# An encoder layer in split fp32: the mixer's weights split in the first input stage and kept in DRAM

## Chip, cores, metric

The kernel runs on one core of a Trainium2 chip. The metric is the device time of one execution in microseconds, the median of several.

## What is computed

One layer on x (1024 tokens, 1024 features, fp32) and a condition vector c. Three sub-layers follow each other, each

```
x <- LayerNorm(ALPHA * x + w * (1 + gate(c)) * f(x * (1 + scale(c)) + shift(c)))

1. f = SwiGLU FFN, w = 1/2:      (silu(h @ Wg) * (h @ Wu)) @ W_out,   2816 hidden columns
2. f = mixer, w = 1:             proj = h @ mix_w_in  (1024 x 2560: glu_a, glu_b, q, k, v)
       conv_out = silu(LN(depthwise_conv31(glu_a * sigmoid(glu_b))))        512 features
       attn_out = 4 heads of differential attention, partial rotary         512 features
       f = concat(conv_out, attn_out) @ mix_w_out                           1024 x 1024
3. f = SwiGLU FFN, w = 1/2
```

All shifts, scales and gates are one product of silu(c) with w_ada (1024 x 9216).

## The kernel before

Products run in a split form: each fp32 operand x is stored as `hi` (x rounded to fp32r, an ACT cast, L139) and `lo` (x minus hi, a subtract, L140), and a product is three matmuls, hi with hi, lo with hi, hi with lo. The helper `split` makes such a pair; its subtract is on DVE unless another engine is named.

The stages, in the order of time: (a) the first input stage (`in_phase`, profile lines L305 to L473): 22 steps j, each of which makes 128 hidden columns of gate and up. A step is a Strassen-Winograd product with seven products of half size (A11, A12, A22, S1 to S4 in the names). Its weights are loaded as tiles `ra` and `rb`, four sums of tiles are made (`sf`, L329 to L332), and both are split (`ah`/`al` and `sh`/`sl`). The sums of the activations (`r_0t` and so on, L264 to L272) are made on POOL, chunk by chunk (0 to 3), as the condition's columns for the chunk come in (`ada0a`, DVE, L708 and L710) and `A`, `B` (L724, L725) are made from them. (b) The first output stage (`out_phase`, L563). (c) The mixer's projections: glu (L891), then k, q, v (`proj_tok`), while DVE runs the convolution (L910). (d) Attention, 32 iterations, each of scores, softmax (maximum on DVE, L1036; exponential on ACT, L1038), `combine` (DVE makes `c`, POOL scales and adds the two maps, L1089 and L1090), transposes of p and the product with v. (e) The output projection (L1274). (f) The second FFN's two stages.

A list scheduler places the instructions of each engine in one order; each engine then executes its queue in order and waits at the head. A tile pool with `bufs` tiles of a tag hands a tile out again when its last readers are done.

What the change touches: in stage (b) a hook makes the second gate, `gate1` (`ada_gate`: eight accumulations on DVE, L151 and L153, for each of two halves). In (c) the weights of mix_w_in are loaded raw (`glur`, `kr`, `qr`, `vr`, 20 tiles of 128x1024) and split by ACT and DVE. In (d) and (e) `out_weights` loads the eight tiles of mix_w_out (`mor`), multiplies each by gate1 (L1060; tiles 0, 1, 6, 7 on POOL, 2 to 5 on DVE) and splits it (`moh`, `mol`). In (a) a hook after each step from j=2 on makes parts of the condition's columns and gates (`ada`, DVE).

Of the kernel before, what the change touches and what calls it, by code (L numbers as in the profile page):

```python
# [48 lines left out]
def layer_kernel(ctx, tc, a, out):  # L49
# [239 lines left out]
    def new_ops():  # L289
# [4 lines left out]
        "ra": ([P, 3, 4, P], 2), "rb": ([P, 4, P], 2), "ah": ([P, 3, 4, P], 2), "al": ([P, 3, 4, P], 2),  # L294
# [11 lines left out]
    def in_load(wp, s, w_in, j):  # L306
        rp = raw_pool.get(s, wp)
        ra = rp.tile([P, 3, 4, P], F32, tag="ra", bufs=2, name=f"ra{s}_{j}")
        rb = rp.tile([P, 4, P], F32, tag="rb", bufs=2, name=f"rb{s}_{j}")
# [5 lines left out]
        return ra, rb  # L315

    def in_gate(wp, s, j, raws):
        ra, rb = raws
        ah = wp.tile([P, 3, 4, P], F32R, tag="ah", bufs=2, name=f"ah{s}_{j}")
        al = wp.tile([P, 3, 4, P], F32R, tag="al", bufs=2, name=f"al{s}_{j}")  # L320
        split(ah, al, ra)
        return {n: (ah[:, i], al[:, i]) for i, n in enumerate(("A11", "A12", "A22"))}

    def in_sums(wp, s, j, raws, left, eng=V, order=(0, 1)):
        ra, rb = raws
        if s == 2 and order == (0, 1) and j in (1, 2):
            eng = G
        sf = [wp.tile([P, 2, 4, P], F32, tag="sf", bufs=2, name=f"sf{s}_{j}_{i}") for i in range(2)]
        eng.tensor_tensor(sf[0][:, 0], rb, ra[:, 2], ALU.add)  # L329
        eng.tensor_tensor(sf[0][:, 1], sf[0][:, 0], ra[:, 0], ALU.subtract)  # L330
        eng.tensor_tensor(sf[1][:, 0], ra[:, 0], rb, ALU.subtract)
        eng.tensor_tensor(sf[1][:, 1], ra[:, 1], sf[0][:, 1], ALU.subtract)  # L332
        for i in order:
            sh = wp.tile([P, 2, 4, P], F32R, tag="sh", bufs=3, name=f"sh{s}_{j}_{i}")
            sl = wp.tile([P, 2, 4, P], F32R, tag="sl", bufs=3, name=f"sl{s}_{j}_{i}")
            split(sh, sl, sf[i])
            for e in range(2):
                left[f"S{2 * i + e + 1}"] = (sh[:, e], sl[:, e])
# [172 lines left out]
    def out_phase(s, wp, w_out, gd, gate, xs, done, after, hook):  # L511
# [111 lines left out]
        for i, (n, k) in enumerate(steps):  # L623
# [15 lines left out]
            if k < cut:  # L639
# [9 lines left out]
                hook(n, k)  # L649
# [16 lines left out]

    x_in = a["x"][0]
    with pool("p1a") as wp:
        in_tags(wp, "ra rb ah al sf sh sl")
# [138 lines left out]
    rows = tc.alloc_tile_pool(name="rows", bufs=1, reuse_waits="tile", side="right")  # L808
    gate1 = rows.tile([P, D], F32, tag="gate1", name="gate1")
    mix_in = a["mix_w_in"][0]  # L810
    spill1 = [dram.tile([P, D], F32, name=f"spill1_{t}", tag="spill1", bufs=NT) for t in range(NT)]
    hm = [[None, None] for _ in range(KD)]
    with pool("p1b") as wp:
# [24 lines left out]

        def load_glu(wp, i, th, tl, nb, tr, nr):
            ws = []  # L840
            for kh in range(2):
                raw = wp.tile([P, 4, 2 * P], F32, tag=tr, bufs=nr, name=f"glur{i}{kh}")
                src = mix_in[kh * H : (kh + 1) * H, :].rearrange("(k p) n -> p k n", p=P)
                SY.dma_start(raw[:, :, 0:P], src[:, :, i * P : (i + 1) * P])
                SY.dma_start(raw[:, :, P : 2 * P], src[:, :, H + i * P : H + (i + 1) * P])
                if th:
                    hi = wp.tile([P, 4, 2 * P], F32R, tag=th, bufs=nb, name=f"gluh{i}{kh}")
                    lo = wp.tile([P, 4, 2 * P], F32R, tag=tl, bufs=nb, name=f"glul{i}{kh}")
                else:
                    hi, lo = slot(f"gluh{i}{kh}", (P, 4, 2 * P)), slot(f"glul{i}{kh}", (P, 4, 2 * P))  # L850
                split(hi, lo, raw)
# [615 lines left out]
```

## Time and profile before

| | us |
|---|---|
| median of 3 runs (lowest, highest) | 1918.4 (1914.31, 1918.53) |
| profiled execution, its time | 1915.77 |
| its span, first to last instruction | 1914.0 |
| TensorE busy in it | 1828.2 |
| VectorE busy | 1463.4 |
| ScalarE busy | 773.6 |
| GpSimd busy | 325.6 |

The span is that of the profiled execution. PE is TensorE's matmuls, DVE is VectorE, ACT is ScalarE, POOL is GpSimd, SP is the engine that issues most transfers. Busy time counts the work, not the issue of transfers by SP; time in which PE is not busy is where it waits. The mean granted clock of TensorE is 0.979.

### The profile page before, as it was taken

What the parts mean: (1) busy time and instruction counts of PE and PEld (TensorE: products, weight loads), DVE (VectorE), ACT (ScalarE), POOL (GpSimd) and SP (SyncE); (2) the same over time, 40 slices, a digit from 0 to 9 for tenths busy, and PEclk for the clock granted to TensorE, in tenths of its full rate; (3) what the DMA queues carried; (4) which work ended last, traced back from release to release, by engine and by line L of the source; (5) the groups of instructions that cost most, each with busy time, mean ns of one, the idle gap of its engine ahead of it and who ended that gap; (6) DMA issues with size and microseconds to landing.
All of it is one profiled execution on the core that took longest, in us unless ns stands there. A gap on an engine that the chain in (4) does not pass through costs nothing. (4 is left out here: it accounts for less than half of the span.)

```text
span 1914.0 us, 23141 instructions
## 1 busy us (share of the span) xinstructions
PE 1828.2 (96%) x8562; PEld 1513.0 (79%) x8562; DVE 1463.4 (76%) x1982; ACT 773.6 (40%) x1233; POOL 325.6 (17%) x259
## 2 busy tenths in 40 slices
PE   5899999999999999999999889979999999999997
PEld 5688888888888878878788677857888888888886
DVE  8867667766698878999888768688777565569888
ACT  3423333332445442133277664353333333354540
POOL 3200000000000020057667541260000000000001
PEclk7899999999999999999999999989999999999999
DMA  8536555442885324111000014125555333188432
GB/s 254 165 99 208 163 161 175 158 149 83 296 301 165 113 61 163 46 35 33 11 2 1 12 45 154 67 67 170 168 172 177 121 110 127 39 285 281 127 121 72
DMA packets 203696, 246.76 MB, mean 129 GB/s; under 512 B 14122, under 2 KB 124831, under 8 KB 203582
## 3 DMA queue, kind: packets, MB, share of 16 engines
q1 hardware_dynamic: 200234, 235.81, 38.6%
q0 software_dynamic: 2112, 7.34, 1.0%
q10 hardware_dynamic: 1236, 2.13, 0.3%
q8 instruction: 67, 1.10, 0.2%
q14 instruction: 47, 0.39, 0.1%
HBM read 188.08 MB, written 57.15 MB: 128 GB/s over the span
## 5 line engine op out<-in xcount | busy, mean ns | idle before, releaser
L563 PE MATMUL fo<-wr,gl 128*128 128x512 f32 x1848 | 422.5, 390 | 0.5 <-DVE pv L606 0.4
L563 PEld LDWEIGHTS fo<-wr,gl 128*128 128x128 f32 x1848 | 346.2, 188 | 74.8 <-DVE pv L606 0.8
L140 DVE TENSOR_TENSOR sl<-sf,sh 128x1024 fp32r<-128x1024 f32 x87 | 109.3, 1257 | 118.5 <-ACT sh L139 118.5
L139 ACT CAST sh<-sf 128x1024 fp32r<-128x1024 f32 x88 | 92.7, 1054 | 210.0 <-issue 35.8
L910 DVE SCALAR_TENSOR_TENSOR cacc<-u,convw,cacc 128x1009 f32<-128x1009 f32 (+14 forms) x120 | 151.5, 1324 | 0.2
L373 POOL DMA_DIRECT2D gd<-gf x8 | 4.6, 573 | 824.4 <-DVE gf L439 823.9
L140 DVE TENSOR_TENSOR gl<-gr,gl 128x512 fp32r<-128x512 f32 x148 | 102.3, 698 | 7.2 <-ACT gl L139 5.8
L139 ACT CAST gl<-gr 128x512 fp32r<-128x512 f32 x148 | 90.5, 618 | 23.2 <-DMA gr<-gd 16.5
L153 DVE SCALAR_TENSOR_TENSOR ada<-adaw,c_act,ada 128x512 f32<-128x512 f32 x98 | 73.3, 748 | 32.9 <-DMA adaw<-in_w_ada_dram 31.9
L215 POOL TENSOR_TENSOR rr<-rv,mhalf 128x1 f32<-128x1 f32 x24 | 21.8, 909 | 410.3 <-DVE rv L213 408.9
L1036 DVE TENSOR_REDUCE mx<-sc 128x1 f32<-128x1024 f32 x64 | 76.3, 1216 | 19.2 <-PE sc L1034 19.2
L1038 ACT ACTIVATE p<-sc,mx 128x1024 f32<-128x1024 f32 x64 | 71.6, 1122 | 45.1 <-DVE mx L1036 44.9
L139 ACT CAST ah<-ra 128x1536 fp32r<-128x1536 f32 x44 | 65.1, 1479 | 58.0 <-DMA ra<-in_ffn_w_in_dram 14.3
L140 DVE TENSOR_TENSOR al<-ra,ah 128x1536 fp32r<-128x1536 f32 x44 | 77.1, 1752 | 1.6 <-ACT ah L139 1.4
L401 ACT ACTIVATE gf<-gf 128x512 f32<-128x512 f32 x44 | 27.8, 632 | 120.8 <-DVE gf L400 114.9
L139 ACT CAST wr<-wa 128x512 fp32r<-128x512 f32 x66 | 41.2, 624 | 74.3 <-PE fo L563 73.7
L140 DVE TENSOR_TENSOR wr<-wa,wr 128x512 fp32r<-128x512 f32 x66 | 45.5, 690 | 26.6 <-ACT wr L139 26.3
L891 PE MATMUL glu<-hm,gluh 128*128 128x512 f32 x256 | 65.6, 391 | 0.0
L1090 POOL TENSOR_TENSOR p<-p,p 128x1024 f32<-128x1024 f32 x27 | 65.0, 2408 | 1.8
L139 ACT CAST wr<-wb 128x512 fp32r<-128x512 f32 x66 | 40.2, 620 | 60.4 <-PE fo L563 49.7
L1107 PE MATMUL av<-vf,aT 128*128 128x128 f32 x512 | 63.2, 277 | 1.0 <-ACT cacc L1172 1.0
L1107 PEld LDWEIGHTS av<-vf,aT 128*128 128x128 f32 x512 | 60.6, 194 | 1.5 <-ACT cacc L1172 1.3
(3490 smaller groups left out, 4735.9 us busy)
## 6 DMA issues: line engine op xcount, KB each, us to landing
gr<-gd SPq DMA_DIRECT2D x148, 256.0 KB, 3.4
ra<-in_ffn_w_in_dram SPq DMA_DIRECT2D x132, 256.0 KB, 3.7
adaw<-in_w_ada_dram SPq DMA_DIRECT2D x56, 512.0 KB, 3.9
gd<-gf SPq DMA_DIRECT2D x102, 256.0 KB, 2.1
rb<-in_ffn_w_in_dram SPq DMA_DIRECT2D x44, 256.0 KB, 3.7
wb<-in_ffn_w_out_dram SPq DMA_DIRECT2D x44, 256.0 KB, 5.0
wa<-in_ffn_w_out_dram SPq DMA_DIRECT2D x44, 256.0 KB, 5.1
gd<-s SPq DMA_DIRECT2D x40, 256.0 KB, 2.0
```

The source lines that it names most:

```text
L139: a = S.copy(hi, x)
L140: b = eng.tensor_tensor(lo, x, hi.bitcast(F32), ALU.subtract)
L153: V.scalar_tensor_tensor(acc, raw[:, jj], c_act[:, n : n + 1], acc, ALU.mult, ALU.add)
L215: G.tensor_tensor(r, v, mhalf[:, 0:1], ALU.pow)
L401: S.activation(c0, c0, AF.Silu)
L563: PE.matmul(ps, lhsT=g[:, x, ts_], rhs=w[:, y], start=n in (1, 2, 3) and k == i == 0, stop=k == NK - 1 and i == 2, skip_group_check=n not ...
L891: PE.matmul(q[2 * m + h], lhsT=w[:, m * P : (m + 1) * P], rhs=hm[k][h][:, x], start=k == 0 and n == 0, stop=k == KD - 1 and n == 2,)
L910: V.scalar_tensor_tensor(acc[:, lo_t:hi_t], u[:, lo_t + sh : hi_t + sh], convw[:, i, jj : jj + 1], acc[:, lo_t:hi_t], ALU.mult, ALU.add,)
L1036: V.tensor_reduce(mx_, ps, axis=AX.X, op=ALU.max, negate=True)
L1038: S.activation(pe, ps, AF.Exp, bias=mx_, accum_out=sm[:, e : e + 1])
L1090: last = G.tensor_tensor(p0, p0, p1, ALU.add)
L1107: PE.matmul(ps[:, 0:P], lhsT=aT[:, kt], rhs=vf[kt][:, h * P : (h + 1) * P], start=kt == 0, stop=kt == 7)
```

## The change

The split of the mixer's weights is taken out of stages (c) to (e) and made in stage (a), in 56 units of 128x512 (40 of mix_w_in, 16 of mix_w_out): POOL's queue loads the weights, for mix_w_out DVE multiplies them by gate1, ACT makes the rounded part, DVE subtracts in place, POOL's queue stores both parts to DRAM (`mwi`, `mwo`). Two tiles (`mw`) are in turn; a step makes two units where it also works on the condition's columns, and four otherwise. The mixer then loads hi and lo from DRAM with SP, two transfers for one. gate1 is made in stage (a) at j=3 and 5, and the late constants are loaded at j=7 in place of 3. The four tile sums of a step in stage (a) are made in place in one tile of four (`r4`), so that the separate `sf` tiles go, and they come after `al` has read the tile. The pools for hi and lo in (c) grow from 4 to 5 tiles.

```diff
     def in_load(wp, s, w_in, j):
         rp = raw_pool.get(s, wp)
-        ra = rp.tile([P, 3, 4, P], F32, tag="ra", bufs=2, name=f"ra{s}_{j}")
-        rb = rp.tile([P, 4, P], F32, tag="rb", bufs=2, name=f"rb{s}_{j}")
+        if s == 0:
+            r4 = rp.tile([P, 4, 4, P], F32, tag="r4", bufs=2, name=f"r4{s}_{j}")
+            ra, rb = r4[:, 0:3], r4[:, 3]
...
     def in_sums(wp, s, j, raws, left, eng=V, order=(0, 1)):
...
+        if s == 0:
+            for i in order:
+                if i == 0:
+                    eng.tensor_tensor(ra[:, 2], rb, ra[:, 2], ALU.add)
+                    eng.tensor_tensor(rb, ra[:, 0], rb, ALU.subtract)
+                    eng.tensor_tensor(ra[:, 0], ra[:, 2], ra[:, 0], ALU.subtract)
+                else:
+                    eng.tensor_tensor(ra[:, 1], ra[:, 1], ra[:, 0], ALU.subtract)
...
-            split(sh, sl, sf[i])
+            split(sh, sl, r4[:, i::2] if s == 0 else sf[i])
...
+        gate1_at = (3, 5)
...
+        def mix_part(src, dst, gate=None):
+            t = wp.tile([P, 2, H], F32, tag="mw", bufs=2, name="mw")
+            G.dma_start(t[:, 0], src)
+            if gate is not None:
+                V.tensor_tensor(t[:, 0], t[:, 0], gate, ALU.mult)
+            S.copy(t[:, 1].bitcast(F32R), t[:, 0])
+            V.tensor_tensor(t[:, 0].bitcast(F32R), t[:, 0], t[:, 1], ALU.subtract)
+            G.dma_start(dst, t)
...
         def hook(j):
-            if j == 3:
-                late_consts(wp, "ra", 2)
+            if j in gate1_at:
...
+                todo[j + 1] = ada_gate(wp, raw_slot, 1, 1.0, mods["gate1"], n)
+            if j == 7:
+                late_consts(wp, "r4", 2)
...
+            for _ in range(2 if j in cols_at + gate_at + gate1_at else 4):
+                if units:
+                    src, dst, *hs = units.pop(0)
+                    mix_part(src, dst, mods["gate1"][:, hs[0]] if hs else None)
...
-        def hook(gi, j):
-            if (gi, j) in ((5, 3), (7, 3)):
-                todo1[(7, 2) if gi == 5 else (4, 1)] = ada_gate(wp, raw_ar, 1, 1.0, gate1, int(gi == 7))
...
-                raw = wp.tile([P, 4, 2 * P], F32, tag=tr, bufs=nr, name=f"glur{i}{kh}")
...
-                split(hi, lo, raw)
+                for g in range(2):
+                    src = mwi[g][kh * H : (kh + 1) * H].rearrange("(k p) x n -> p k x n", p=P)
+                    for x, w in enumerate((lo, hi)):
+                        SY.dma_start(w[:, :, g * P : (g + 1) * P].bitcast(F32), src[:, :, x, i * P : (i + 1) * P])
...
-                SY.dma_start(raw, src)
...
-                split(hi, lo, raw)
...
+                src = mwi[col // H][q * 256 : (q + 1) * 256].rearrange("(k p) x n -> p k x n", p=P)
+                for x, w in enumerate((lo, hi)):
+                    SY.dma_start(w.bitcast(F32), src[:, :, x])
...
-    def out_weights(wp, j, eng=V, tag="raw", size=D):
-        raw = wp.tile([P, size], F32, tag=tag, bufs=2, name=f"mor{j}")[:, 0:D]
-        SY.dma_start(raw, a["mix_w_out"][0, j * P : (j + 1) * P, :])
-        eng.tensor_tensor(raw, raw, gate1, ALU.mult)
+    def out_weights(j):
         mo_w[j] = slot(f"moh{j}", (P, D)), slot(f"mol{j}", (P, D))
-        split(*mo_w[j], raw)
+        for w, x in zip(mo_w[j], (1, 0)):
+            SY.dma_start(w.bitcast(F32).rearrange("p (h n) -> p h n", h=2), mwo[j][:, :, x])
...
-            last = combine(i)
+            combine(i)
...
-                with tc.issue_after(last):
-                    out_weights(wp, (i - 22) // 4, G)
+                out_weights((i - 22) // 4)
```

The order of instructions, first on POOL at the start of the program. The names end in buffer numbers; `r0_0t12` and `r0_0t34` are the tile sums of the activations' chunk 0, which the profile shows as `r_0t`. Before:

```order
masks.py:197 MEMSET ident_73 128x128
L87 MEMSET mhalf_80 128x4
masks.py:199 ISA
masks.py:199 AFFINE_SELECT ident_73<-ident_73 128x128
L264 TENSOR_TENSOR r0_0t12_278<-h0_0_1_267,h0_0_0_255 128x512
L265 TENSOR_TENSOR r0_0t12_278<-h0_0_1_267,r0_0t12_278 128x512
L271 TENSOR_TENSOR r0_0t34_285<-h0_0_1_267 128x512
L272 TENSOR_TENSOR r0_0t34_285<-h0_0_0_255,r0_0t12_278 128x512
```

Of the change, from the same row:

```order
masks.py:197 MEMSET ident_73 128x128
L87 MEMSET mhalf_80 128x4
L814 DMA mw_965<-in_mix_w_in_dram 128x512
masks.py:199 ISA
masks.py:199 AFFINE_SELECT ident_73<-ident_73 128x128
L819 DMA mwi0_99<-mw_965 128x1024
L814 DMA mw_970<-in_mix_w_in_dram 128x512
L814 DMA mw_1129<-in_mix_w_in_dram 128x512
L819 DMA mwi0_99<-mw_970 128x1024
L819 DMA mwi0_99<-mw_1129 128x1024
L814 DMA mw_1134<-in_mix_w_in_dram 128x512
L264 TENSOR_TENSOR r0_0t12_292<-h0_0_1_281,h0_0_0_269 128x512
```

Three stores and four loads (`mw`) stand ahead of the first sum, and one more load ahead of the second; a load of a tile waits until the store of two units ago has landed, and a store waits for its subtract.

Then on DVE at the same place, from the making of `A` and `B` for chunk 0 on (`sf` and `r4` hold the sums of the first step's weights, `h` is the activation). Before:

```order
L724 TENSOR_TENSOR B0_107<-ada0p0_193,bada_84 128x2
L725 SCALAR_TENSOR_TENSOR A0_106<-ada0p0_193,bada_84 128x2
L329 TENSOR_TENSOR sf0_0_0_385<-rb0_0_225,ra0_0_224 128x512
L331 TENSOR_TENSOR sf0_0_1_386<-ra0_0_224,rb0_0_225 128x512
L330 TENSOR_TENSOR sf0_0_0_385<-sf0_0_0_385,ra0_0_224 128x512
L140 TENSOR_TENSOR al0_0_235<-ra0_0_224,ah0_0_234 128x1536
L740 TENSOR_SCALAR h0_0_0_255<-hT0_0_0_246,A0_106,B0_107 128x512
L332 TENSOR_TENSOR sf0_0_1_386<-ra0_0_224,sf0_0_0_385 128x512
L740 TENSOR_SCALAR h0_0_1_267<-hT0_0_1_258,A0_106,B0_107 128x512
```

Of the change:

```order
L743 TENSOR_TENSOR B0_122<-ada0p0_208,bada_84 128x2
L744 SCALAR_TENSOR_TENSOR A0_121<-ada0p0_208,bada_84 128x2
L140 TENSOR_TENSOR al0_0_249<-r40_0_239,ah0_0_248 128x1536
L818 TENSOR_TENSOR mw_970<-mw_970 128x512
L336 TENSOR_TENSOR r40_0_239<-r40_0_239 128x512
L759 TENSOR_SCALAR h0_0_0_269<-hT0_0_0_260,A0_121,B0_122 128x512
L759 TENSOR_SCALAR h0_0_1_281<-hT0_0_1_272,A0_121,B0_122 128x512
L337 TENSOR_TENSOR r40_0_239<-r40_0_239 128x512
L818 TENSOR_TENSOR mw_1129<-mw_1129 128x512
L338 TENSOR_TENSOR r40_0_239<-r40_0_239 128x512
L340 TENSOR_TENSOR r40_0_239<-r40_0_239 128x512
```

`al0_0` moved ahead of the sums, which now write into its operand, and two subtracts of units (L818) stand among them; one more stands before this piece and others follow.

Last on POOL in the attention, around the tile `mor0` (`p` are the attention maps, `c` their factors, `r44` the factor of an output tile). Before:

```order
L1090 TENSOR_TENSOR p220_8760<-p220_8760,p221_8769 128x1024
L1126 TENSOR_TENSOR r44_8803<-ss4_8568,mhalf_80 128x4
L1060 TENSOR_TENSOR mor0_8875<-mor0_8875,gate1_3723 128x1024
L1089 TENSOR_SCALAR p231_8837<-p231_8837,c123_8884 128x1024
L1090 TENSOR_TENSOR p230_8828<-p230_8828,p231_8837 128x1024
L1089 TENSOR_SCALAR p241_8905<-p241_8905,c124_8963 128x1024
```

Of the change:

```order
L1119 TENSOR_TENSOR p220_8969<-p220_8969,p221_8978 128x1024
L1155 TENSOR_TENSOR r44_9012<-ss4_8777,mhalf_80 128x4
L1118 TENSOR_SCALAR p231_9046<-p231_9046,c123_9090 128x1024
L1119 TENSOR_TENSOR p230_9037<-p230_9037,p231_9046 128x1024
L1118 TENSOR_SCALAR p241_9111<-p241_9111,c124_9169 128x1024
L1119 TENSOR_TENSOR p240_9102<-p240_9102,p241_9111 128x1024
```

The multiply of `mor0` is gone, and the rest stands as it did.

## Rows read from the trace of the kernel before

**Rows 1.** Page, busy us (share of the span) and instructions.

```profile
PE 1828.2 (96%) x8562; PEld 1513.0 (79%) x8562; DVE 1463.4 (76%) x1982; ACT 773.6 (40%) x1233; POOL 325.6 (17%) x259
```

**Rows 2.** Windows: length, busy of each engine (instructions), clock, DMA share, GB/s.

```profile
22.00:52.00 30.00, 19.90 (x71) 15.95 (x71) 29.64 (x45) 12.93 (x17) 11.32 (x8) 0.56 0.73 229
106.00:490.00 384.00, 383.39 (x1718) 316.48 (x1717) 261.54 (x370) 124.58 (x159) 0.00 (x0) 1.00 0.48 151
490.00:640.00 150.00, 150.00 (x663) 123.94 (x662) 124.53 (x198) 77.55 (x137) 4.72 (x7) 1.00 0.74 243
850.00:950.00 100.00, 94.32 (x431) 77.99 (x430) 95.03 (x79) 24.23 (x47) 75.29 (x55) 0.97 0.09 27
1050.00:1200.00 150.00, 129.47 (x769) 110.37 (x769) 112.38 (x146) 90.75 (x184) 57.84 (x33) 0.95 0.20 67
```

**Rows 3.** DVE timeline, 0 to 60 us: start, length, work [idle before].

```profile
15.62 1.75 DVE L140 TENSOR_TENSOR al<-ra,ah 128x1536 fp32r<-128x1536 f32 x1
...
20.82 0.95 DVE L708 TENSOR_SCALAR ada0a<-ada,c_act 128x256 f32<-128x256 f32 x1 [1.04 <-DMA ada<-in_w_ada_dram]
```

**Rows 4.** POOL timeline, 0 to 80 us.

```profile
19.00 1.28 POOL L264 TENSOR_TENSOR r_0t<-h,h 128x512 f32<-128x512 f32 x1 [17.70 <-ACT h L251]
```

**Rows 5.** DMA, 0 to 90 us: 40 slices; issues with KB, us to landing.

```profile
GB/s 18 278 360 350 294 316 349 349 346 348 348 349 349 348 277 11 0 250 354 95 0 256 305 293 351 312 259 146 0 0 0 0 39 226 209 134 292 116 44 23
...
ada<-in_w_ada_dram SPq DMA_DIRECT2D x16, 512.0 KB, 8.4
```

**Rows 6.** Page, costliest groups: busy, mean ns | idle before.

```profile
L373 POOL DMA_DIRECT2D gd<-gf x8 | 4.6, 573 | 824.4 <-DVE gf L439 823.9
L140 DVE TENSOR_TENSOR gl<-gr,gl 128x512 fp32r<-128x512 f32 x148 | 102.3, 698 | 7.2 <-ACT gl L139 5.8
```

**Rows 7.** DMA issues, the whole span: KB each, us to landing.

```profile
gd<-gf SPq DMA_DIRECT2D x102, 256.0 KB, 2.1
...
spill<-x POOLq DMA_DIRECT2D x8, 512.0 KB, 3.0
...
gd<-gf POOLq DMA_DIRECT2D x8, 256.0 KB, 3.4
```

**Rows 8.** Groups by line, 106 to 490 us.

```profile
L140 DVE TENSOR_TENSOR sl<-sf,sh 128x1024 fp32r<-128x1024 f32 x37 | 45.2, 1222 | 53.2 <-ACT sh L139 53.2
...
L401 ACT ACTIVATE gf<-gf 128x512 f32<-128x512 f32 x20 | 12.7, 633 | 55.6 <-DVE gf L400 55.6
```

**Rows 9.** PE waits, 800 to 950 us: total, times, longest.

```profile
PE kT L982 <- DVE khl L140: 2.6, 2, 2.2
PE qTh L1018 <- POOL qh L1005: 1.8, 1, 1.8
PE qTl L1018 <- POOL ql L1006: 1.7, 1, 1.7
```

**Rows 10.** POOL timeline, 870 to 940 us.

```profile
877.95 11.81 POOL L956 TENSOR_TENSOR rcq<-qf,ropec 128x128 f32<-128x128 f32 x1 [12.14 <-ACT qf L988]
...
893.64 1.44 POOL L956 TENSOR_TENSOR rcq<-qf,ropec 128x128 f32<-128x128 f32 x1
```

**Rows 11.** PE waits, 1075 to 1125 us.

```profile
PE aT L247 <- POOL p L1090: 6.7, 2, 6.0
PE qTh L1018 <- DVE aT L1099: 2.6, 1, 2.6
PE aT L247 <- DVE r L1083: 2.5, 1, 2.5
```

**Rows 12.** Groups by line, DVE, 1075 to 1130 us.

```profile
L1129 DVE TENSOR_TENSOR o<-o,r 128x512 f32<-128x512 f32 x2 | 5.7, 2852 | 5.1 <-POOL r L1126 5.1
...
L1060 DVE TENSOR_TENSOR mor<-mor,gate 128x1024 f32<-128x1024 f32 x2 | 4.4, 2192 | 0.0
L140 DVE TENSOR_TENSOR mol<-mor,moh 128x1024 fp32r<-128x1024 f32 x2 | 4.3, 2140 | 0.0
```

**Rows 13.** Groups by line, POOL, 1060 to 1200 us.

```profile
L1060 POOL TENSOR_TENSOR mor<-mor,gate 128x1024 f32<-128x1024 f32 x4 | 10.5, 2616 | 31.0 <-DVE x L1280 29.8 <-DVE fl L140 1.2
```

More of the change, by code (lines that the diff above doesn't have):

```diff
@@ L314, in in_load @@
             SY.dma_start(dst, src)
-        return ra, rb
+        return ra, rb, r4
     def in_gate(wp, s, j, raws):
-        ra, rb = raws
+        ra, _, _ = raws
         ah = wp.tile([P, 3, 4, P], F32R, tag="ah", bufs=2, name=f"ah{s}_{j}")
@@ L324, in in_sums @@
     def in_sums(wp, s, j, raws, left, eng=V, order=(0, 1)):
-        ra, rb = raws
+        ra, rb, r4 = raws
         if s == 2 and order == (0, 1) and j in (1, 2):
             eng = G
[L328 to L332, printed above, removed]
+        if s == 0:
[4 more added lines that the diff above has]
+                    eng.tensor_tensor(ra[:, 0], ra[:, 2], ra[:, 0], ALU.subtract)
+                else:
+                    eng.tensor_tensor(ra[:, 1], ra[:, 1], ra[:, 0], ALU.subtract)
+        else:
+            sf = [wp.tile([P, 2, 4, P], F32, tag="sf", bufs=2, name=f"sf{s}_{j}_{i}") for i in range(2)]
+            eng.tensor_tensor(sf[0][:, 0], rb, ra[:, 2], ALU.add)
+            eng.tensor_tensor(sf[0][:, 1], sf[0][:, 0], ra[:, 0], ALU.subtract)
+            eng.tensor_tensor(sf[1][:, 0], ra[:, 0], rb, ALU.subtract)
+            eng.tensor_tensor(sf[1][:, 1], ra[:, 1], sf[0][:, 1], ALU.subtract)
         for i in order:
@@ L506, in in_phase, with out_phase @@
         return gd
-    def out_phase(s, wp, w_out, gd, gate, xs, done, after, hook):
+    def out_phase(s, wp, w_out, gd, gate, xs, done, after):
         wp.tile([P, H], F32, tag="gr", bufs=4, name="gr_")
@@ L664, in out_phase @@
             after(1, k)
+    rows = tc.alloc_tile_pool(name="rows", bufs=1, reuse_waits="tile", side="right")
     x_in = a["x"][0]
+    mix_in = a["mix_w_in"][0]
+    mwi = [dram.tile([D, 2, H], F32, name=f"mwi{g}", tag="mwi", bufs=5) for g in range(5)]
+    mwo = [dram.tile([P, 2, 2, H], F32, name=f"mwo{j}", tag="mwo", bufs=8) for j in range(8)]
     with pool("p1a") as wp:
-        in_tags(wp, "ra rb ah al sf sh sl")
+        in_tags(wp, "r4 ah al mw sh sl")
         ops = new_ops()
@@ L789, in layer_kernel @@
         gate_at = (16, 18)
+        gate1_at = (3, 5)
         todo = {}
-        def hook(j):
-            if j == 3:
-                late_consts(wp, "ra", 2)
+        def mix_part(src, dst, gate=None):
[6 more added lines that the diff above has]
+            G.dma_start(dst, t)
+        units = []
+        for g in range(5):
+            for k in range(KD):
+                ks = slice(k * P, (k + 1) * P)
+                units.append((mix_in[ks, g * H : (g + 1) * H], mwi[g][ks]))
+        for j in range(8):
+            for h in range(2):
+                hs = slice(h * H, (h + 1) * H)
+                units.append((a["mix_w_out"][0, j * P : (j + 1) * P, hs], mwo[j][:, h], hs))
+        def hook(j):
+            if j in gate1_at:
+                n = gate1_at.index(j)
+                if n == 0:
+                    mods["gate1"] = rows.tile([P, D], F32, tag="gate1", name="gate1")
+                todo[j + 1] = ada_gate(wp, raw_slot, 1, 1.0, mods["gate1"], n)
+            if j == 7:
+                late_consts(wp, "r4", 2)
             if j in cols_at:
@@ L1215, in layer_kernel @@
         for j in (2, 3):
-            out_weights(wp, j)
+            out_weights(j)
     qfp.release()
```

51 lines of the change are left out of this document (20 added, 31 removed).

## Prediction

> **What bounds the kernel now.** I read the busy row of the page first, then the windows by stage, then in each stage that the change touches the list of what PE waits for, and last the rows of single operations for prices. TensorE works 1828.2 of 1914.0 us [rows 1], so all that a change of the other engines can win lies in the 86 us in which PE stands. The windows [rows 2] say where they are. In the steady part of the first input stage PE works 383.39 of 384 us and in the first output stage 150.00 of 150: nothing can be won there, only lost. In the start, from 22 to 52 us, PE works 19.90 of 30 us, and there VectorE is the one without a gap (29.64 of 30). In the projections of the mixer (850 to 950) PE misses 5.7 us of 100, with DVE at 95.03. In the last third of the attention and the start of the output projection (1050 to 1200) it misses 20.5 us of 150, and no other engine is full (DVE 112.38, ACT 90.75, POOL 57.84): this is a chain of waits, not a full engine.
>
> So the change adds work in two places (a start that DVE bounds, and a stage that PE fills), and takes it away in two where PE waits.
>
> **The units.** 56 units are added, 40 for the input weights, 16 for the output weights: a load and a store on POOL's queue, an ACT copy and a DVE subtract of 128x512, and for 16 of them a DVE multiply. By the nearest rows [rows 6] one unit costs DVE 0.698 and POOL two issues of 0.573 us, and I give ACT's copy DVE's 0.7; all together DVE and ACT 39 us each, POOL 64.2, and 56 x 0.786 MB (256 KB in, 512 KB out) = 44 MB. POOL is idle from 106 to 490 us (0.00 busy, [rows 2]), so its 64 us cost nothing there; what counts is where the units stand in the queues.
>
> **Start: +8 us (bounds +2.5 and +14).** The code makes the units from step 2 on, but the order shows ten of them before the first product of step 0 is drained, five of these ahead of the second part of chunk 0. They cost in two ways.
> First, DVE: five subtracts fall in the stretch that it fills, 5 x 0.698 = 3.5 us, less the 1.04 us that it waited for a transfer before it [rows 3]: +2.5 is the lower bound.
> Second, POOL. It makes the tile sums of the activations (r_0t at 19.00 for 1.28, its second operation behind it at 20.3, [rows 4]), and now stands in between at loads and stores that wait. The walk for chunk 0: the subtract of the second unit stands behind al0_0, which ended at 15.62 + 1.75 = 17.4 [rows 3], so near 18 us; its store is issued at 18.7 and lands 3.0 later (the price of a 512 KB store on this queue, [rows 7]), at 21.7; only then is the load in front of r_0t free to go, and r_0t starts near 22.3, 3.3 late. Its second operation stands behind one more load, which waits for the store of the third unit, whose subtract stands behind the sums and both h: about 21.5 + 0.6 + 3.0 + 0.6 = 25.7 in place of 20.3, 5.4 late. The store in front of r_0t34 waits for a subtract behind r_0bl, some 2 us later still. The next chunks repeat this with the later units. Bytes add to it: three stores and five loads ahead of that point are 2.9 MB, 8.3 us at the 349 GB/s at which DMA is full until 34 us [rows 5], of which perhaps half is ahead of a piece that DVE waits for. These overlap; I take +8, since DVE has no gaps in which to make up the 5 to 7 us. If each of two chained stores lands in 8.4 us, as the loads of this stretch do [rows 5], and not in 3.0, 8 + 2 x 5.4 = 18.8, of which I hold back what the bytes term already counted (4.2): +14 is the upper bound.
>
> **Input stage, steady: +3 us (bounds 0 and +16).** DVE gets the subtracts of 46 units, 16 multiplies and 16 accumulations of the second gate, moved here, 78 x 0.698 = 54.4 us more, 261.5 + 54.4 = 315.9 of 384, or 82%. The output stage shows 124.53 of 150, also 83%, with PE at 150.00 [rows 2], so the load alone need not hold PE; and 53.2 us of DVE's idle time here is waiting for ACT [rows 8], which no product waited for. The danger is the queue: a subtract at DVE's head waits for an ACT copy, that for a load, that for the store of two units ago, and behind it stand the drains of PE's banks. One round trip is 0.573 + 3.4 + 0.7 + 0.698 + 0.573 + 3.0 = 8.9 us [rows 6, 7], with two tiles 4.4 us a unit. A step is 384/20 = 19.2 us (20 of the sigmoids of a step in this window, L401, [rows 8]): four units need 17.7, two need 8.9. That fits, with 1.5 us to spare in the five or so steps that make four. If the landings are longer by half (3.2 us a trip), four units need 24, 5 us too many in five steps, of which a part is made up: 5 x 3.2 = 16 is the upper bound. I take 3, nearer the side where it fits.
> The sums in place are the same four operations; a tile is held until its parts are made, about one step, and two tiles are in turn as before, with DMA at 48% of its time [rows 2]. The gate's 16 operations leave the output stage, where PE is full. Both: 0.
>
> **Mixer's projections: -4 us (bounds -1 and -7).** 20 subtracts of 128x1024 leave DVE, about 24 us of work, and 20 ACT copies. PE's waits there are kT for khl 2.6, qT for POOL's qh and ql 1.8 + 1.7, 6.1 in all [rows 9]. The first goes: khl stands behind such subtracts. The other two end a chain of 32 POOL operations whose first took 11.81 us where the next of its form takes 1.44 [rows 10], while DVE was 95% busy. It goes only as far as that hold shortens. Twice the bytes are loaded, where DMA is busy 9% [rows 2]: 0.
>
> **Attention, last third: -10 us (bounds -5 and -14).** Between 1075 and 1125 us PE waits 6.7 us for POOL's p, 2.6 for aT's copy, 2.5 for r on DVE [rows 11]. POOL multiplies the output weights there (2.616 us each, [rows 13]), twice right behind the r that DVE's `o` waits for. `o`, beside it, takes 2.852 for 512 columns, where the same form without such company takes 0.70 [rows 6, 12]: +2.15, twice. DVE itself does two multiplies (2.192) and two subtracts (2.140) of these weights among the softmax's maxima and the copies aT [rows 12]: 2 x (2.15 + 2.19 + 2.14) = 13 us on DVE in 55, on a chain of DVE, ACT, POOL and PE in turn. All gone would be the 11.8 us of these waits and a little clock (0.95 from 1050 to 1200, [rows 2]): -14. One stall with its subtract, the rest covered by other work, is 2.15 + 2.14 = 4.3, and something of the second: -5. I take 10, nearer the waits than the floor, since the longest of them, 6.0, is for POOL's p, which this DVE and POOL work holds up on both sides.
>
> **Output projection: -1 us (0 to -2).** The last four weight tiles lose their multiplies, two on POOL at 2.616 [rows 13], but these stood beside products; of the 20.5 us of the whole stretch [rows 2] the waits above are 11.8, and little of the rest lies there.
>
> Sum: 8 + 3 - 4 - 10 - 1 = -4. The profiled execution took 1915.77, 2.6 under the median shown; the mean of the four is 1916.8. 1916.8 - 4 = 1912.8; I say 1912.5. By the ends of the terms: 1916.8 - 21.5 = 1895 to 1916.8 + 24 = 1941.
>
> **A rule that speaks against it.** A store of 256 KB to gd issued by SP lands in 2.1 us, the same store from POOL's queue in 3.4 [rows 7], 1.3 more. The Trainium skill, "SBUF — State Buffer", section "SBUF: two separate sides", says that descriptors of transfers issued by GpSimd are written by its own cores, and that certain DVE operations lock these out until they end. The rows agree in sign; no row shows 112 such transfers under a DVE at 83%. By the rule a trip would be longer by what is left of the DVE operation at each of its two issues, at most the 1.75 us of the longest, al [rows 3]: 8.9 + 3.5 = 12.4, 25 us for four units, which is the second rival below.
>
> **Rivals.** *The start decides* (slower). POOL's queue holds the sums of every chunk by two full landings, the start costs 14 and the steps 6; attention gives 7, projections and output 4: 1916.8 + 20 - 11 = 1926. For it: POOL stands in order, and the first ten units sit in the one stretch where DMA, DVE and POOL are all needed. Against: PE has 10 us of its own idle time there, but it waits for the same chunks. It decides from a start that is more than 12 us late.
> *The transfers hold the steps* (slower). POOL's preparation of a transfer is held as the 11.81 us operation was (10 us over the next); trips of 12 us make the steps lose 16 by the bound above: 1916.8 + 8 + 16 - 15 = 1926. Against: 8.3 us a unit are to be had on the average (384/46), so two tiles allow a trip of 16.7.
> *The start is hidden* (faster). +2.5, steps 0, all of attention and most of the projections: 1916.8 + 2.5 - 13 - 5 = 1901.
> *Attention doesn't give it back* (no change). Its chain waits for latency, another wait ends last: -4, projections -2: 1916.8 + 8 + 2 - 6 = 1921.
> That the change does not do what it says I leave out: in the order the subtracts, multiplies and copies are gone from DVE, POOL and ACT.
>
> **How the numbers follow.** The forecast, 1906 to 1919, has 0.40; the start decides 0.19; transfers hold 0.08; hidden 0.21; no return 0.12. 0.3% of the median, 5.75 us, is what a measurement of this kernel can tell from no change, so faster means under 1912.6, slower over 1924.2. Faster is half the forecast and the hidden start, 0.41; slower the first two rivals and a little of the last, 0.28; same the rest, 0.31. The range leaves out the ends beyond the first and third rivals: 1899 to 1928.
>
> **What would show it.** Right: PE's unbroken work begins some 8 us later; r_0t starts after 22 us; DVE near 82% between 106 and 490 us with at most 4 us of PE waits; no wait of PE over 3 us for p or aT between 1075 and 1130. Wrong: a PE wait for a product's bank in most steps, or a start over 12 us late (slower); r_0t at 19 us as before and PE's start less than 3 us late (faster); waits for c and p of the old length in the attention (no gain).

## The result and the profile after

The changed kernel takes 1981.97 us (median of 4 runs, 1978.78 to 1984.16), the kernel before 1917.88 in the same comparison. The ratio is 1.0337, 95% interval 1.0318 to 1.0356: 64 us slower, where 4 to 5 us faster was forecast, and outside the range.

The first product of step 2, of the output stage, of glu, of the scores and of the output projection cut the span into pieces. The view of one tile gives the start of its first product; for the changed kernel, for example, in the first and the second of these:

```profile
L367 PE MATMUL fi_2A<-r_0bh,ah x4: 389/389/389, 119.7 to 1376.6; 128*128 128x512 f32 x4
```

```profile
L578 PE MATMUL fo<-wr,gl x1848: 387/389/504, 581.8 to 1968.7; 128*128 128x512 f32 x185
```

The same views of both kernels give this table (us, profiled executions).

| piece | before | after | difference | forecast |
|---|---|---|---|---|
| start, to the first product of step 2 | 102.1 | 119.7 | +17.6 | +8 |
| steps 2 to 21, to the first product of the output stage | 392.3 | 462.1 | +69.8 | +3 |
| output stage, to glu | 215.9 | 214.0 | -1.9 | 0 |
| projections, to the first scores | 232.3 | 230.3 | -2.0 | -4 |
| attention, to the output projection | 209.4 | 193.3 | -16.1 | -10 |
| the rest | 762.0 | 761.1 | -0.9 | -1 |

So the gains came, 19 us in the last three rows for 15 forecast, and the steps took 70 us in place of 3. The windows of the changed kernel, at the stages that [rows 2] show of before (length, busy of each engine, clock, DMA share, GB/s):

```profile
22.00:52.00 30.00, 19.16 (x80) 15.18 (x80) 26.84 (x40) 10.97 (x15) 13.62 (x14) 0.67 0.98 334
124.00:578.00 454.00, 409.17 (x1723) 330.72 (x1722) 312.39 (x451) 149.04 (x205) 47.45 (x87) 0.94 0.66 217
580.00:730.00 150.00, 150.00 (x662) 123.97 (x661) 120.48 (x190) 78.23 (x139) 5.18 (x7) 1.00 0.66 217
935.00:1035.00 100.00, 94.81 (x438) 78.03 (x437) 75.64 (x66) 20.02 (x44) 72.69 (x53) 0.98 0.14 43
1118.00:1268.00 150.00, 142.06 (x898) 124.27 (x898) 105.05 (x157) 95.74 (x208) 58.95 (x39) 0.99 0.29 99
```

In the steps PE was busy 383.39 of 384 us [rows 2]; now 409.17 of 454, at a granted clock of 0.94 in place of 1.00. DVE is at 69% there (312.39 of 454), not at the 82% of the forecast: it isn't full. It works 51 us more than the 261.54 of [rows 2], near the 54 of the forecast, but in a longer time. From 1118 to 1268 PE works 142.06 of 150 us, where [rows 2] had 129.47.

PE stands in 16 places of this window, 44.8 us in all. The longest of these waits (total, times, longest):

```profile
PE fi_2A L367 <- ACT p L409: 8.2, 1, 8.2
PE fi_11A L367 <- ACT p L409: 5.2, 1, 5.2
PE fi_5A L367 <- ACT p L409: 4.7, 1, 4.7
PE fi_8A L367 <- DVE gf L473: 3.3, 1, 3.3
```

These are copies on ACT that drain PE's banks (p, L409; u, L423) and sums on DVE behind such work. And ACT, in the same stretch:

```profile
ACT mw L817 <- DMA mw<-in_mix_w_in_dram: 84.5, 23, 8.6
...
ACT mw L817 <- DVE mw L816: 24.8, 8, 7.9
```

ACT stands 84.5 us in 23 places at the rounding of a unit whose load has not landed, and 24.8 us at units that DVE has not yet multiplied. POOL, the third queue:

```profile
POOL mwi L819 <- DVE mw L818: 78.2, 16, 16.3
POOL mw L814 <- DMA mwi<-mw: 60.8, 22, 7.3
POOL mwo L819 <- DVE mw L818: 53.2, 11, 11.7
```

POOL stands at stores that wait for DVE's subtract, and at loads that wait for a store's landing. One tile's trip, on POOL, and ACT beside it (start, length, work [idle before]):

```profile
264.26 0.55 POOL L814 DMA_DIRECT2D mw<-in_mix_w_in_dram  x1 [2.78 <-DMA mwi<-mw]
...
270.39 0.54 POOL L819 DMA_DIRECT2D mwi<-mw  x1 [1.84 <-DVE mw L818]
278.28 0.54 POOL L814 DMA_DIRECT2D mw<-in_mix_w_in_dram  x1 [7.34 <-DMA mwi<-mw]
```

```profile
268.65 0.62 ACT L817 CAST mw<-mw 128x512 fp32r<-128x512 f32 x1 [4.59 <-DMA mw<-in_mix_w_in_dram]
...
283.81 0.62 ACT L817 CAST mw<-mw 128x512 fp32r<-128x512 f32 x1 [7.05 <-DMA mw<-in_mix_w_in_dram]
284.33 1.47 ACT L139 CAST ah<-r 128x1536 fp32r<-128x1536 f32 x1
285.71 0.58 ACT L423 COPY u<-fi_8A 128x512 f32<-128x512 f32 x1
```

The load is issued at 264.26 and rounded at 268.65, the store issued at 270.39, and the next load into this tile only at 278.28, when the store has landed: a trip of 14.0 us, for 8.9 in the forecast. Most of the excess is this store's landing, 7.9 us for 3.0; the median of such stores in the steps is 4.4 us. The load of 278.28 is rounded at 283.81, after ACT has stood 7.05 us for it. Behind it in ACT's queue stand the rounding `ah` and then u, the copy that empties the bank of a product of step 8, and PE waits for u:

```profile
286.34 0.50 PE L367 MATMUL fi_8A<-r_0t3h,sh 128*128 128x512 f32 x1 [2.46 <-ACT u L423]
```

So one landing of a store holds POOL's next load, that load ACT's rounding, the rounding a drain, and the drain PE. The longest wait of PE, 8.2 us up to 133.54, is of the same kind: ACT stood 8.63 and 1.98 us at two roundings for their loads, and the copy p came behind them. In eleven of the thirteen waits of PE over 1 us ACT has stood at the rounding of a unit just before. The second way to PE is through DVE, whose subtract waits for the rounding, with the sum that PE needs behind it:

```profile
269.30 0.69 DVE L818 TENSOR_TENSOR mw<-mw 128x512 fp32r<-128x512 f32 x1 [3.78 <-ACT mw L817]
...
270.51 0.68 DVE L473 TENSOR_TENSOR gf<-gf,fi_7A 128x512 f32<-128x512 f32 x1
```

Such a wait can cost twice. PE after the wait for this sum:

```profile
271.24 0.79 PE L367 MATMUL fi_8A<-r_0bh,ah 128*128 128x512 f32 x1 [3.28 <-DVE gf L473]
271.83 0.63 PE L367 MATMUL fi_8A<-r_0bl,ah 128*128 128x512 f32 x1
...
274.38 0.40 PE L367 MATMUL fi_8A<-r_2bl,ah 128*128 128x512 f32 x1
274.61 0.40 PE L367 MATMUL fi_8A<-r_2bh,al 128*128 128x512 f32 x1
```

After a wait of 3.28 us the products take 0.63 us, up to 274.38, and then 0.40. The granted clock is 0.50 from 271.3 to 274.3 us, the lower of its two levels (1.2 GHz), and 1.00 from 274.7 on, the higher (2.4 GHz). Not each wait is followed by it: after those of 1.50 and 1.12 us the products stay at 0.40. Of the 70 us in the steps some 45 (454 less 409.17) are PE standing. The other 25 are nearly the same number of products (1723, and 1718 in [rows 2]), some 110 of them slowed as here.

### The profile page after: what moved, and what is told of

The parts are those of the page before. It is cut to its first block, busy times and chain, and to the rows that moved or that the text cites. A ratio compares the mean times of both kernels' runs of the same rounds, so it can differ in the third digit from the quotient of the medians.

```text
span 1980.5 us, 23567 instructions
## 1 busy us (share of the span) xinstructions
PE 1850.8 (93%) x8562; PEld 1524.9 (77%) x8562; DVE 1462.4 (74%) x2022; ACT 774.4 (39%) x1261; POOL 375.2 (19%) x367
## 5 line engine op out<-in xcount | busy, mean ns | idle before, releaser
L943 DVE SCALAR_TENSOR_TENSOR cacc<-u,convw,cacc 128x1014 f32<-128x1014 f32 (+14 forms) x120 | 146.4, 1288 | 0.2
L139 ACT CAST gl<-gr 128x512 fp32r<-128x512 f32 x148 | 90.5, 617 | 21.5 <-DMA gr<-gd 15.0
L140 DVE TENSOR_TENSOR sl<-sf,sh 128x1024 fp32r<-128x1024 f32 x43 | 54.5, 1267 | 59.5 <-ACT sh L139 59.5
L817 ACT CAST mw<-mw 128x512 fp32r<-128x512 f32 x56 | 34.7, 620 | 155.8 <-DMA mw<-in_mix_w_in_dram 108.7
L139 ACT CAST sh<-sf 128x1024 fp32r<-128x1024 f32 x44 | 46.4, 1054 | 104.5 <-issue 8.2
L1070 ACT ACTIVATE p<-sc,mx 128x1024 f32<-128x1024 f32 x64 | 71.5, 1118 | 36.2 <-DVE mx L1068 36.1
L140 DVE TENSOR_TENSOR sl<-r,sh 128x1024 fp32r<-128x1024 f32 x44 | 54.5, 1244 | 21.5 <-ACT sh L139 21.2
L818 DVE TENSOR_TENSOR mw<-mw 128x512 fp32r<-128x512 f32 x56 | 38.2, 685 | 35.8 <-ACT mw L817 35.5
```

What stands on the lines that cost most here:

```text
L139: a = S.copy(hi, x)
L140: b = eng.tensor_tensor(lo, x, hi.bitcast(F32), ALU.subtract)
L818: V.tensor_tensor(t[:, 0].bitcast(F32R), t[:, 0], t[:, 1], ALU.subtract)
L943: V.scalar_tensor_tensor(acc[:, lo_t:hi_t], u[:, lo_t + sh : hi_t + sh], convw[:, i, jj : jj + 1], acc[:, lo_t:hi_t], ALU.mult, ALU.add,)
L1070: S.activation(pe, ps, AF.Exp, bias=mx_, accum_out=sm[:, e : e + 1])
```

## The experiments

Each time stands beside runs of the kernel before on the same chip, whose medians are 1915.5 to 1917.35 us. A time given with a ratio is the median of several executions, and one without a ratio is a single execution. "Start" and "steps" are the first two rows of the table, in the changed kernel 119.7 and 462.1.

**The mixer's part alone.** The units are left out; the mixer's loads read one block that is made once.

```diff
             for _ in range(2 if j in cols_at + gate_at + gate1_at else 4):
-                if units:
+                if False:
...
-                    src = mwi[g][kh * H : (kh + 1) * H].rearrange("(k p) x n -> p k x n", p=P)
+                    src = mwi[0][kh * H : (kh + 1) * H].rearrange("(k p) x n -> p k x n", p=P)
```

> Leaves out the 56 units; the mixer's loads of both parts read one block of split weights that is made once at step 17, so they move the same bytes as the changed kernel but other weights. Sums in place and the second gate's move stay. If the units alone made the loss, the start is back (first product of step 2 near 102 us, 119.7 in the changed kernel), the steps take 392 us from there to the first product of the output stage (462 in the changed kernel), and the gain of the mixer (-2, -2 and -16 us in the changed trace) stands alone: about 1898 us, 1893 to 1904. If the sums in place or the gate's move cost something in the steps, the time is 1910 or more.

Measured: 1898.27 us, ratio 0.9913 (0.9897 to 0.9930); start 104.0, steps 394.2. The units made the whole loss, 84 us. What is left of the change in the first stage (sums in place, the second gate, and the one block made here) costs 2 us in the start and 2 in the steps. With these counted, the change without its units gains 17 us.

**The units held until after the start.** The first load of a unit is queued on POOL behind the last tile sum of the activations.

```diff
-            G.dma_start(t[:, 0], src)
+            with tc.issue_after(held[0]):
+                G.dma_start(t[:, 0], src)
```

> Holds the first unit's load on POOL's queue behind the last tile sum of the start; everything else is the changed kernel. If the ten early units made the start late, the first product of step 2 comes back to 102 to 106 us and the steps stay 70 us too long: about 1967 us. The rival, that the same 56 units in fewer steps only shift the loss, gives steps that are 10 us longer still and 1975 us or more.

Measured: 1971.96 us, start 103.9, steps 469.1. The start is back, so the early units made 15.8 of its 17.6 us. But the steps are 7 us longer: part of that loss only moved, as the rival had it, and the time lies between the two forecasts.

**The units' work without their transfers.** Loads and stores are left out; copies, subtracts and multiplies run on two tiles set once.

```diff
-            t = wp.tile([P, 2, H], F32, tag="mw", bufs=2, name="mw")
-            G.dma_start(t[:, 0], src)
+            t = mwt[len(units) % 2]
...
-            G.dma_start(dst, t)
```

> Keeps the units' ACT copies, DVE subtracts and multiplies, 56 of each kind as before, but leaves out their loads and stores (they work on two tiles set once; the mixer reads one block as in the first run). If the loss in the steps is waiting for transfers at the head of ACT's queue, it goes: steps of 392 to 400 us, total 1900 to 1912 us. If it is the work itself, DVE at over 80% and ACT's copies between the drains, the steps stay 30 us or more too long: 1930 us or more.

Measured: 1908.22 us, start 112.0 (units are not held here), steps 396.1. Its window over the steps:

```profile
112.00:508.00 396.00, 393.40 (x1758) 324.26 (x1757) 308.45 (x443) 143.12 (x192) 0.05 (x1) 1.00 0.54 176
```

DVE is at 308.45 of 396 us, 78%, and PE works 393.40. Without transfers to wait for, more of the work runs early: 26 of the 56 subtracts fall into this window (44 in that of the changed kernel), the others into the start, which is 8 us longer than with the mixer's part alone. So the work of all 56 units costs 10 us over the mixer's part alone, for 84 with the transfers. That 44 units' work fits into the steps this run does not show; the transfers, and the waiting for them, make the larger part of the loss.

**A unit's stores left out**, all else as in the held version (the mixer reads one block).

```diff
-            G.dma_start(dst, t)
```

> All 56 units, held until after the start, with loads, copies, subtracts and multiplies, but without their stores (the mixer reads one block that is stored apart at step 17). In the changed kernel a tile's trip took 14 us, of which the store's landing and the wait for it are about 8. Without it a trip is 0.55 + 4.4 + 0.7 + 0.7 = 6.4 us, two tiles give a unit every 3.2 us, and four units fit a step of 19.2 us: steps of 392 to 410 us, 1898 to 1918 us in all. If it were the loads themselves that ACT waits for, each as long as it takes to land, the steps stay 30 us too long or more: 1930 us and up.

Measured: 1945.6 us, start 104.2, steps 441.4: over the bound, and in the range that was given for the loads themselves being what ACT waits for. The stores carry 28 of the held version's 75 us over the mixer's part alone; 47 stay without them. A shorter trip helps, then, but is not enough: POOL and ACT still wait on each other through DVE.

```profile
POOL mw L817 <- DVE mw L821: 199.9, 38, 19.3
```

```profile
ACT mw L820 <- DMA mw<-in_mix_w_in_dram: 67.3, 27, 7.8
```

A load now waits only for the subtract of the tile's last unit, but that stands in DVE's queue in its turn, the load goes out late, and the next rounding stands at ACT's head again, 67.3 us in all.

**Place in the queue: the pair that decides.** Both make 38 units, two a step, held until after the start, with the same transfers and operations (the mixer reads one block of them). In the first, load in one step and round a step later:

```diff
+        def mix_part(t, dst, gate=None):
+            with tc.issue_after(act_at[0]), tc.issue_after(dve_at[0]):
...
+                S.copy(t[:, 1].bitcast(F32R), t[:, 0])
+                V.tensor_tensor(t[:, 0].bitcast(F32R), t[:, 0], t[:, 1], ALU.subtract)
+            G.dma_start(dst, t)
...
+            while loaded:
+                mix_part(*loaded.pop(0))
+            if j < 21:
+                for _ in range(2):
+                    loaded.append(mix_load(*units.pop(0)))
```

> 38 of the units, two in each step from j=2 on, the rest left out (the mixer reads one block of them). The load is issued in one step, and copy and subtract stand a step later in ACT's and DVE's queues, behind the copy p5 and the sum p7 of that step. The transfers and the work are those of the next kernel, only the place in the queues differs. If waiting at the head of the queue is the cause, the steps take 392 to 400 us and the time is 1897 to 1908 us. If trips of 14 us or DMA contention cost in themselves, it is as slow as the next kernel.

In the second the scheduler places the rounding, as in the changed kernel:

```diff
+            if j > 2:
+                for _ in range(2):
+                    mix_part(*units.pop(0))
```

> The same 38 units, two in each step from j=3 on, with copy and subtract placed where the scheduler puts them, as in the changed kernel. By the queue theory copies again wait for loads at the head of ACT's queue; two units a step leave a trip of 14 us some slack, so 15 to 45 us are lost in the steps: 1912 to 1945 us. If only the number of units in a step mattered, two would fit and it is 1897 to 1908 us like the one before.

Measured: 1907.12 us with the step between, steps 402.0; 1959.84 without, steps 454.1. The roundings of the units on ACT, first with and then without the step between (busy, mean ns | idle before):

```profile
L826 ACT CAST mw<-mw 128x512 fp32r<-128x512 f32 x38 | 22.2, 621 | 0.6 <-DMA mw<-in_mix_w_in_dram 0.6
```

```profile
L820 ACT CAST mw<-mw 128x512 fp32r<-128x512 f32 x36 | 22.4, 621 | 114.4 <-DMA mw<-in_mix_w_in_dram 114.3
```

and the transfers (median us to landing), in the same order:

```profile
mwi<-mw POOLq DMA_DIRECT2D x36, 512.0 KB, 6.0
...
mw<-in_mix_w_in_dram POOLq DMA_DIRECT2D x36, 256.0 KB, 4.4
```

```profile
mwi<-mw POOLq DMA_DIRECT2D x36, 512.0 KB, 3.9
...
mw<-in_mix_w_in_dram POOLq DMA_DIRECT2D x35, 256.0 KB, 4.1
```

With the step between, ACT idles 0.6 us at the roundings, and 114.4 without; the steps differ by 52 us. (With 402.0 they are still 8 us longer than without units, and 2 over the forecast.) The transfers are not faster in the fast kernel: the stores land in 6.0 us there and in 3.9 in the slow one. The second run lost more with two units a step than was expected: 60 us over the mixer's part alone, for 75 in the held version with all 56 units. Making only two a step does not make them fit; with the same number, placing them a step later takes 52 of the 60 us away.

**Units wholly on POOL**, so that nothing of them stands in ACT's or DVE's queue; first as written, then with the third gate's load queued later on SP.

```diff
-                V.tensor_tensor(t[:, 0], t[:, 0], gate, ALU.mult)
-            S.copy(t[:, 1].bitcast(F32R), t[:, 0])
-            V.tensor_tensor(t[:, 0].bitcast(F32R), t[:, 0], t[:, 1], ALU.subtract)
+                G.tensor_tensor(t[:, 0], t[:, 0], gate, ALU.mult)
+            G.tensor_scalar(t[:, 1].bitcast(F32R), t[:, 0], 1.0, 0.0, ALU.mult, ALU.add)
+            G.tensor_tensor(t[:, 0].bitcast(F32R), t[:, 0], t[:, 1], ALU.subtract)
```

> All of a unit on POOL: load, multiply, rounding, subtract, store, held behind the last tile sum of the start. Nothing of a unit then stands in ACT's or DVE's queue. If waiting at the head of ACT's queue is the cause, the steps take 392 to 402 us and the time is 1898 to 1910 us, under the kernel before. The rival: POOL's operations hold DVE's beside them, as POOL's multiply did to o in the attention (2.85 for 0.70 us); 128 such operations at 1.3 to 2 us each cost the steps 20 us or more: 1920 us or more.

```diff
+                with tc.issue_after(lastload[0]):
+                    todo2[j + 2] = ada_gate(wp, raw_slot, 2, 0.5, mods["gate2"], (j - 10) // 3)
```

> The units wholly on POOL as in the second kernel of that name, but the third gate's load is queued on SP behind the second FFN's weights. There it stood early in SP's queue and waited 97 us for POOL's last multiply, since the third gate reuses the second's tile, and SP's later loads waited behind it. Without that wait of 89 us on DVE the time should fall to 1936 us, 1928 to 1944. What then stays over 1898 us is POOL's operations holding DVE's beside them (the accumulations took 0.88 us there for 0.745): if that were nothing, 1898 to 1910 us.

Measured: 2026.15 us (ratio 1.0583, 1.0554 to 1.0613), and 1956.94. Both missed the forecast times; the first came out slower than 1920, as its rival had it, but for another reason in the main. In it, one wait of DVE makes more than half of the 128 us over the mixer's part alone (69 us, by the second run):

```profile
441.08 0.43 DVE L192 TENSOR_SCALAR gate<-gate 128x512 f32<-128x512 f32 x1 [88.98 <-DMA gate<-in_b_ada_dram]
```

The third gate's tile is the second's; its load stood early in SP's queue and waited for POOL's last multiply, and with it SP's next loads. Without that the steps are still 441.8 us, and DVE's operations are longer beside POOL's:

```profile
L153 DVE SCALAR_TENSOR_TENSOR ada<-adaw,c_act,ada 128x512 f32<-128x512 f32 x78 | 76.3, 978 | 20.6 <-DMA adaw<-in_w_ada_dram 20.4
```

This form took 0.745 us on the changed kernel's page, and takes 0.978 here. The windows over the steps, of the mixer's part alone and then of this run:

```profile
104.00:498.00 394.00, 393.14 (x1757) 324.02 (x1756) 283.24 (x399) 129.10 (x165) 0.00 (x0) 1.00 0.51 166
```

```profile
110.00:555.00 445.00, 412.64 (x1773) 334.07 (x1772) 336.21 (x405) 132.15 (x172) 201.04 (x222) 0.97 0.71 238
```

Nearly the same operations take DVE 336 us in place of 283. POOL does not wait for ACT any more, but DVE is slower beside it. This was priced at 38 us over the mixer's part alone, and the run is 59 over it. That the slower DVE makes all of the 59 is likely but not shown: DVE also waits longer for its transfers there.

**Where the attention's gain came from.** The kernel before, once without the multiplies by the second gate, once with POOL's four given to DVE.

```diff
-        eng.tensor_tensor(raw, raw, gate1, ALU.mult)
```

> The kernel before without the multiply of the output weights by the second gate (left out altogether); their rounding and subtracts stay. If the multiplies, POOL's two beside o and DVE's, were the larger part of the 16 us that the change won before the output projection, the stretch from the first scores to the output projection falls from 209 us to 197 to 202, and the time is 1904 to 1910 us. If the subtracts and ACT copies were, it stays over 204 us and the time over 1911 us.

```diff
-                    out_weights(wp, (i - 22) // 4, G)
+                    out_weights(wp, (i - 22) // 4)
...
-                    out_weights(wp, j, V if j < 6 else G, "ah", 3 * H)
+                    out_weights(wp, j, V, "ah", 3 * H)
```

> The kernel before with POOL's four multiplies given to DVE, 1.2 us each for 2.6. If POOL's multiply cost by holding DVE's o beside it and POOL's own scaling of p behind it, the stretch falls by 4 to 10 us and the time is 1906 to 1912 us. If DVE's sum of work in this stretch is what counts, DVE gets 2.4 us more there and loses 4.3 us of holding: 1914 to 1919 us.

Measured: 1908.13 us, ratio 0.9956 (0.9941 to 0.9971), the stretch 202.5 us; and 1912.47, ratio 0.9979 (0.9970 to 0.9989), the stretch 204.1. The multiplies are 6.9 of the 16.1 us, just outside the range for their being the larger part; by difference the splits, and what else changed in the order there, are the other 9; no run leaves out the splits alone. Moving POOL's to DVE alone gives 5.3 us of the stretch, though DVE then gets two more multiplies in it: what cost was POOL's multiply, by holding DVE or by standing before POOL's own work on p. The hold is shown: `o` takes 0.691 us in that run, for the 2.852 of [rows 12]. The stretch comes from the fastest of ten executions (1909.35 us); their median lies 0.5 over the forecast time. Without the multiplies PE's wait on r is gone, that on POOL's p is down from the 6.7 of [rows 11], and that on the copy aT stays:

```profile
PE aT L247 <- POOL p L1089: 3.8, 2, 3.4
PE qTh L1018 <- DVE aT L1098: 2.7, 1, 2.7
```

**Only the output weights' units.** Only the 16 units of the output weights are made in the first input stage, one a step, rounded a step after the load; the input weights are split in the mixer as before.

```diff
+            while loaded:
+                mix_part(*loaded.pop(0))
+            if units and j >= 5:
+                src, dst, hs = units.pop(0)
+                loaded.append(mix_load(src, dst, mods["gate1"][:, hs]))
```

> A version that may beat both: only the 16 units of the output weights are made in the first input stage, one in a step from j=5, with copy and subtract a step after the load; the input weights are split in the mixer as before. The sums in place and the second gate's move stay. The gain before the output projection (16 us in the changed trace) should come alone, with 0 to 4 us lost in start and steps: 1898 to 1905 us. If the gain there came from the input weights' part of the change, it is 1912 us or more.

Measured: 1901.47 us, ratio 0.9914 (0.9894 to 0.9933) to the kernel before. Start 103.5, steps 395.3, attention 193.9 us. Over the steps PE is full:

```profile
104.00:498.00 394.00, 392.27 (x1753) 323.07 (x1752) 301.73 (x427) 137.65 (x180) 16.28 (x30) 1.00 0.59 190
```

It keeps the attention's gain and leaves the 40 units alone that brought 2 us.

## Why the prediction was wrong

*What bounds it, and where the gains are:* right. Nothing could be won in the steps, only lost, and the change without its units gives 17 us. That the gains came to 19 us for 15 is in part luck: the projections gave half of their term and the attention more than its bound.

*The steps, +3 with bounds 0 and +16:* this is the step that failed. The prediction named the place ("a subtract at DVE's head waits for an ACT copy, that for a load, that for the store of two units ago, and behind it stand the drains of PE's banks") and then priced it as a capacity: a trip of 8.9 us, two tiles, "That fits, with 1.5 us to spare" (half of 8.94 is 4.47, so 1.3). A sum of durations holds for a loop whose members start as soon as they can. Here load, rounding, subtract and store stand in three queues that each work in order, at places that the scheduler chose. When one is late, the engine stands, what is behind it is late, and the next unit's load goes out late too. The pair with and without a step between shows it: same work, same transfers, 52 us apart. That trips were longer than 8.9 us (14.0 for the one shown) is part of it, 28 us by the run without stores, but without the stores the steps still lost 47 us over the mixer's part alone. The clock's lower level behind the longer waits, some 25 us, was not in the sum at all.

*The start, +8 with bounds 2.5 and 14:* the mechanism was right and the size off, +17.6. The walk gave r_0t at 22.3 and its second operation at 25.7. POOL's rows of the changed kernel:

```profile
20.37 0.54 POOL L819 DMA_DIRECT2D mwi<-mw  x1 [5.43 <-DVE mw L818]
25.06 0.54 POOL L819 DMA_DIRECT2D mwi<-mw  x1 [4.15 <-DVE mw L818]
27.20 0.56 POOL L814 DMA_DIRECT2D mw<-in_mix_w_in_dram  x1 [1.60 <-DMA mwi<-mw]
27.77 1.27 POOL L264 TENSOR_TENSOR r_0t<-h,h 128x512 f32<-128x512 f32 x1
31.92 0.59 POOL L814 DMA_DIRECT2D mw<-in_mix_w_in_dram  x1 [2.88 <-DMA mwi<-mw]
32.54 1.28 POOL L265 TENSOR_TENSOR r_0t<-h,r_0t 128x512 f32<-128x512 f32 x1
```

27.77 and 32.54. The prediction charged 3.0 us for each store's landing. Here the store issued at 20.37 had landed at 27.20, after 6.8 us, nearer the 8.4 of its upper bound. The walk also left out that the third unit's store stands ahead of r_0t, and not only ahead of its second operation: it went out at 25.06, after its subtract, so r_0t could not have started at 22.3 even with the short landing. The loads and stores of the later chunks added to it. Holding the units gives 15.8 us back.

*Output stage, 0:* -1.9. It is there in the mixer's part alone too, so it is not the units; where in the stage it comes from no run shows. *Mixer's projections, -4:* -2.0, inside the bounds. *Output projection, -1:* -0.9 for all that follows the attention.

*Attention, -10 with bounds -5 and -14:* right in kind, -16.1, outside the bounds. DVE's `o` in the changed kernel, at the place of [rows 12]:

```profile
L1158 DVE TENSOR_TENSOR o<-o,r 128x512 f32<-128x512 f32 x2 | 1.4, 692 | 2.3 <-POOL r L1155 2.3
```

0.692 us for 2.852, and of the waits of [rows 11] on p and r this is left:

```profile
PE aT L247 <- DVE r L1112: 0.3, 1, 0.3
```

The bound was the waits in 50 us and "a little clock". Leaving out the multiplies gives 6.9 us; the other 9, by difference the splits, are more than the waits in that window could show.

*The ends of the sum:* the lower ends add up to -20.5 and not -21.5, so the lower end is 1896 us, not 1895. Nothing hangs on it.

*The rivals:* "The transfers hold the steps" had the place, at a chance of 0.08 and a price of 16 us for 70, and another cause: POOL's preparation of a transfer held by DVE. The issues do not show it. Those in the steps of the changed kernel (mean ns):

```profile
L819 POOL DMA_DIRECT2D mwi<-mw x28 | 15.2, 545 | 121.1 <-DVE mw L818 78.2 <-ACT p L427 9.6 <-DVE ada L153 9.5
L814 POOL DMA_DIRECT2D mw<-in_mix_w_in_dram x27 | 14.8, 546 | 66.4 <-DMA mwi<-mw 55.1 <-DVE ada L153 7.9 <-DVE mw L818 2.8
```

take 0.545 us each, less than the 0.573 of [rows 6]: with DVE at 69%, mostly subtracts and sums, no issue was held. Whether the longer landings (4.4 us for 3.0) hide some of it, no row tells. The Trainium skill in "SBUF — State Buffer", section "SBUF: two separate sides", says that descriptors cannot be written while DVE runs an operation in a two-port mode, and names an fp32 copy as one. The prediction had priced the rule by `al`, a subtract of two inputs; the issue times do not bear this price out. The same section says that a DVE operation with two SBUF inputs and a GpSimd operation that reads SBUF do not run at the same time: the one that starts later waits. With this `o` agrees (2.852 us beside POOL, 0.691 where only POOL's multiplies were moved away), and so do the units on POOL (0.978 for 0.745). "The start decides" was half right: a start over 12 us late, but the smaller of two losses.

## What to carry to other kernels

Work put into the idle time of an engine that others drain through has to be judged by the head of its queue, not by its busy share: ask what stands right behind an instruction that waits for a transfer. If something PE needs stands there, place the instruction so late that its transfer has long landed, a whole step here, and only then count capacity. Before such work goes in, split the gain by its parts: 16 of 56 units brought 16 of 19 us.

## What was not expected of the hardware

A store's landing time does not tell whether anything waits for it: 6.0 us in the kernel that lost 8 us in the steps, 3.9 in the one that lost 60. And 45 us of waits of PE, nearly all in thirteen waits of 1 to 8 us, came with some 110 products slowed to 0.63 us or so from 0.40, at the clock's lower level, so that the loss was 70.
